# Two more gates in a pair, a denser plan for the second mixer, and three pieces of work moved ahead of their waits

## The chip, the cores and the metric

The kernel runs on one core of a Trainium2 chip. The metric is the device time of one execution in microseconds; the figure for a kernel is the median of its runs. The kernel before takes 2862.22 us (three runs, 2858.88 to 2863.82).

## What is computed

One layer of a hybrid decoder, for a prompt of 512 tokens and eight sequences that each add one token. The 520 token columns go through the dense products together. Two token mixers work on the same normalised input, and sigmoid gates merge them; a feed-forward block with a short convolution follows. Cut to what the change touches:

```
mq, mk, mv, mo, mi, mf, fq, fk, fv, ff, ga, gb = split(h @ w_in + b_in)
y_m = mlstm_output(mlstm_fn(q_m, k_m, v_m, ig, lf_m), mo)        # first mixer
q_f, k_f = rmsnorm(fq), rmsnorm(fk); v_f = fv; lf_f = log_sigmoid(ff)
y_f = fox_fn(q_f, k_f, v_f, lf_f)                                # second mixer (FoX), 8 heads of 128
merged = sigmoid(ga) * (y_m @ w_proj_a) + sigmoid(gb) * (y_f @ w_proj_b)
x = x + g1 * (merged @ w_out)
h2 = modulate(rmsnorm(x, norm2_w), sh2, sc2)
a, g = split(h2 @ w_ffn_in)                                      # 2048 -> 2 x 5632
x = x + g2 * ((gelu(conv3(a)) * g) @ w_ffn_out)
```

In the second mixer a prompt token attends to the prompt tokens before it, with a bias from summed log forget values. A sample token attends to 256 past rows, which lie in two pages of 128 rows of a cache (`cache_k`, `cache_v`) that a page table points into, and to itself. `gb` has 2048 channels: 16 tiles of 128 channels, called gates here.

## The kernel before, in words

**Dense products.** Every fp32 operand is split into a high and a low part, and a product is three matmuls (high by high, high by low, low by high). The 520 columns are two halves of 260. For one tile of 128 output channels, `dense` (L196) goes over 16 tiles of 128 input channels: 16 x 3 x 2 = 96 matmuls of 128x260. ScalarE casts a block of 1024 weight columns to its high part `wh` and VectorE subtracts to get the low part `wl` (L167, L168), from a block `raw` that SyncE's queue loads.

**Pairs.** Most products are done by `run_pairs` (L326): two output tiles and two column halves are treated as a 2x2 block product and computed with seven products of 24 matmuls instead of eight. VectorE pays for it with sums of weight blocks (`raw<-raw,raw`) and of results (`tg`, `tt`, `at`). A unit is seven steps, and `late` maps a step to extra work that is issued there. The results of a product of a unit stand in PSUM banks `x`, `y` and `z`; a later product of the unit may write a bank again only when VectorE or ScalarE has read it.

**The second mixer beside the gates.** `NB2` of the 16 gates are computed in pairs, the rest by `dense` in the loop at L1762. `dense` calls `step()` after each of the 16 input tiles, and a step takes the next entry of the list `bg`, which is a plan of the second mixer: entry s holds the functions that are issued after s steps. A step is six matmuls. The plan is written by `put(s, f)` (L1701 to L1732); a scheduler may let an instruction stand later than its step where what it needs comes later. For each of the eight heads, spaced `HP` steps apart from b = 1 + HP*head, the plan issues:

- `f_load` (L1432): five loads `fi` on SyncE's queue; `f_norm` (L1437): two VectorE products `fi<-fi,qwc,fi` and `fi<-fi,nkw,fi`, and a store of the keys by GpSimd (`out_kT`);
- `f_split`: high and low parts, the low parts `fql`, `fkl` on GpSimd; `f_forget` (`nFb`), `f_values` (`vtp`, then `fvl` on VectorE);
- `f_scores` (L1563): four score blocks `fS` on TensorE, softmax on VectorE and ScalarE (`fs`, `sm`); `f_turn` (L1584): transposes `fPT` of the softmax; `f_attend` (`fy`).

For the eight sample tokens the plan issues, sixteen times, `s_load` (L1620): one broadcast load `qb` of the query row from the DRAM scratch `dqf`, on SyncE's queue, and two indirect loads `kp` of a page of keys by GpSimd (`gather`, L868); and `s_scores` (L1630): for each page a product `kp<-kp,qb` and a sum `sc<-kp`, in program order on VectorE. `s_rows` (L1613) writes `dqf` from a transpose `qSt`. After the last score come a softmax (`sS`), its transpose `sPT` (L1659), a `memset` of `pp` on GpSimd, and 32 indirect loads `vp` of pages of values (`s_gather`); each page feeds two matmuls `sO` (`s_attend`, L1682) and then `sOT` and sums into `yS`. `y_split` and `y_sample` make the mixer's result `yf` ready for the product with `w_proj_b` (`pb`).

**The start of the feed-forward block.** `W2` is the last unit of the product with `w_out`. `features(e, z)` (L2098) makes eight input tiles of one column half: for each tile VectorE scales `xa` by the row factor `rr`, the sample columns get a sum (by VectorE for the first tile, by GpSimd for the others), ScalarE writes the high part `bf`, VectorE the low part. Its dictionary `between` names other work that is issued after tile j. `half_norm(z)` makes `rr` of a column half from four sums `ms` on TensorE, through ScalarE and VectorE. `beside` takes the input tiles in turn for several products: `fa` and `fg` are the two halves of FFN unit 0, `fb` is the first of unit 1. Pairs of FFN tiles follow (L2512); `sum_parts(n)` makes eight split tiles from sums of input tiles (eight ScalarE casts `bf<-xa`, eight VectorE differences), and `whole_copy`, `whole_conv`, `whole_gate` finish a tile that was computed without pairing.

**Order on an engine.** Each engine, and SyncE's and GpSimd's queues, runs its instructions in the order in which they stand; an instruction that waits holds all behind it on its engine.

Of the kernel before, what the change touches and what calls it, by code (L numbers as in the profile page):

```python
# [63 lines left out]
def tile_hybrid_step(ctx: ExitStack, tc: tile.TileContext, I, O):  # L64
# [1547 lines left out]

    def s_rows(e):  # L1613
        ps = mm_ps("qSt")
        T.transpose(ps[:32, :P], qS[:, e].rearrange("p b h -> p (b h)"), ident)
        qrow = pt("qrow")
        V.tensor_copy(qrow[:32, :P], ps[:32, :P])
        nc.sync.dma_start(dqf[e].rearrange("b (h d) -> (b h) d", h=4), qrow[:32, :P])

    def s_load(i):  # L1620

        e, b = divmod(i, NS)
        qb = pt("qb")
        nc.sync.dma_start(qb[:, :512], dqf[e, b].partition_broadcast(P))
        kps = [pt("kp") for _ in range(NPG)]
        W.k[i] = qb, kps
        for g, kp in enumerate(kps):
            gather(kp[:, :512], I["cache_k"], idx_h[e][:, b * NPG + g:b * NPG + g + 1])
# [991 lines left out]
```

## Time and profile before

| | before |
|---|---|
| median of three runs | 2862.22 us |
| the profiled execution | 2862.7 us |
| its span, first to last instruction | 2861.0 us |
| TensorE busy | 2825.4 us, 99% |
| VectorE busy | 2154.0 us, 75% |
| ScalarE busy | 1360.5 us, 48% |
| GpSimd busy | 413.3 us, 14% |
| granted TensorE clock, mean | 0.997 |

Times in the text are microseconds from the start of the span. The stages that the change touches: pairs up to 1004.2; the dense gates with the second mixer to about 1215; the products with `w_proj_b` and `w_out` to 1476; the start of the feed-forward block to 1552; then its pairs. In rows of the trace PE is TensorE (PEld its weight loads), DVE VectorE, ACT ScalarE, POOL GpSimd, SP SyncE. A row of a timeline has start, length, engine, line, operation, output and inputs, size and count, and in brackets the idle time just ahead of it and what ended that. Matmul rows overlap: a 128x260 matmul lasts 0.28 us, but the next begins 0.12 us later.

### The profile page before, as it was taken

How to read it: one execution, taken by the hardware profiler on the slowest of the kernel's cores; microseconds unless marked ns; L12 is line 12 of the kernel's file. 1: busy time of each engine (PE TensorE's matmuls, PEld its weight loads, DVE VectorE, ACT ScalarE, POOL GpSimd, SP SyncE). 2: the span in 40 equal slices, each digit the busy share in tenths (PEclk: the TensorE clock that was granted, in tenths of full speed). 3: DMA queues.
4: the chain of work that ended last, by engine and by line, in shares of the span. 5: the costliest groups of instructions: out<-in, count | busy, mean ns of one | idle time of the engine just before them, and what ended most of it. 6: DMA issues, size and time to landing. Idle time of an engine off the chain costs nothing.

```text
span 2861.0 us, 57607 instructions
## 1 busy us (share of the span) xinstructions
PE 2825.4 (99%) x23318; PEld 2711.8 (95%) x23318; DVE 2154.0 (75%) x3318; ACT 1360.5 (48%) x2131; POOL 413.3 (14%) x687
## 2 busy tenths in 40 slices
PE   8999999999999999999999999999999999999999
PEld 6888998999999989799999999999999999999999
DVE  5986764676777759468888887878787888788787
ACT  4335543455455544444555444444444445544543
POOL 0001110211100145402111010101010101100100
PEclk9999999999999999999999999999999999999999
DMA  9946657945555578576772344444343346745753
GB/s 339 308 143 201 232 178 261 302 166 188 195 182 175 182 246 270 183 235 208 216 249 93 127 143 129 156 130 159 129 146 117 127 141 188 208 155 169 189 160 104
DMA packets 226755, 531.44 MB, mean 186 GB/s; under 512 B 30304, under 2 KB 83024, under 8 KB 226488
## 3 DMA queue, kind: packets, MB, share of 16 engines
q1 hardware_dynamic: 187296, 426.89, 46.2%
q0 software_dynamic: 38752, 100.64, 11.5%
q8 instruction: 183, 3.00, 0.4%
q14 instruction: 84, 0.69, 0.1%
q10 hardware_dynamic: 440, 0.23, 0.0%
HBM read 451.28 MB, written 72.92 MB: 183 GB/s over the span
## 4 chain that ended last, share of the span: by engine, by line
PE 85%; DVE 5%; issue 5%; DMA 2%; ACT 2%; POOL 1%; SPq 0%; POOLq 0%; DVEq 0%; ACTq 0%
PE x L60 33%; PE y L60 17%; PE z L60 8%; PE gate L213 4%; PE pre L60 3%; PE fo L60 3%; PE pa L213 3%; PE mo L213 2%; PE adp L60 2%; PE mv L213 2%; PE adp L409 1%; DVE wl L60 1%; PE mq L213 1%; PE mk L213 1%; ACT wh L60 1%
## 5 line engine op out<-in xcount | busy, mean ns | idle before, releaser
L60 DVE TENSOR_TENSOR wl<-raw,wh 128x1024 fp32r<-128x1024 f32 (+1 forms) x666 | 802.1, 1205 | 353.3 <-ACT wh L60 348.6
L60 ACT CAST wh<-raw 128x1024 fp32r<-128x1024 f32 (+1 forms) x666 | 689.5, 1036 | 754.7 <-DVE raw L60 386.3
L60 PE MATMUL x<-bf,wh 128*128 128x260 f32 x2624 | 475.2, 282 | 2.1 <-DVE tg L60 2.1
L60 DVE TENSOR_TENSOR raw<-raw,raw 128x1024 f32<-128x1024 f32 x339 | 413.7, 1220 | 5.8
L60 PEld LDWEIGHTS x<-bf,wh 128*128 128x128 f32 x2624 | 403.3, 188 | 2.2 <-ACT wh L60 2.2
L60 PE MATMUL x<-bf,wl 128*128 128x260 f32 x1312 | 370.0, 282 | 0.0
L60 PEld LDWEIGHTS x<-bf,wl 128*128 128x128 f32 x1312 | 246.8, 188 | 0.0
L60 PE MATMUL y<-bf,wh 128*128 128x260 f32 x1312 | 238.2, 282 | 0.0
L60 PEld LDWEIGHTS y<-bf,wh 128*128 128x128 f32 x1312 | 201.6, 188 | 0.0
L168 DVE TENSOR_TENSOR wl<-raw,wh 128x1024 fp32r<-128x1024 f32 x92 | 113.1, 1229 | 107.8 <-ACT wh L167 105.0
L60 PE MATMUL x<-ff,wh 128*128 128x260 f32 x1024 | 186.1, 283 | 0.0
L60 PE MATMUL x<-hf,wh 128*128 128x260 f32 x1008 | 185.4, 284 | 0.0
L60 PE MATMUL y<-bf,wl 128*128 128x260 f32 x656 | 184.7, 282 | 0.0
L167 ACT CAST wh<-raw 128x1024 fp32r<-128x1024 f32 x92 | 96.4, 1048 | 162.0 <-DMA raw<-in_w_in 43.4
L60 PEld LDWEIGHTS x<-hf,wh 128*128 128x128 f32 x1008 | 155.0, 188 | 13.4 <-issue 7.5
L60 PEld LDWEIGHTS x<-ff,wh 128*128 128x128 f32 x1024 | 157.6, 188 | 0.0
L60 PE MATMUL x<-ff,wl 128*128 128x260 f32 x512 | 144.6, 282 | 0.0
L60 PE MATMUL x<-hf,wl 128*128 128x260 f32 x504 | 142.2, 282 | 0.0
L60 PE MATMUL fo<-fe,wh 128*128 128x260 f32 x768 | 125.6, 284 | 1.1 <-DVE fo L60 0.9
L60 PEld LDWEIGHTS y<-bf,wl 128*128 128x128 f32 x656 | 123.5, 188 | 0.0
L60 PE MATMUL z<-bf,wh 128*128 128x260 f32 x656 | 120.9, 284 | 0.0
L60 PEld LDWEIGHTS fo<-fe,wh 128*128 128x128 f32 x768 | 105.6, 188 | 2.5 <-DVE fo L60 2.1
(642 smaller groups left out, 7076.9 us busy)
## 6 DMA issues: line engine op xcount, KB each, us to landing
raw<-in_w_fi SPq DMA_DIRECT2D x176, 512.0 KB
raw<-in_w_in SPq DMA_DIRECT2D x155, 512.0 KB
ar<-in_w_ada SPq DMA_DIRECT2D x192, 256.0 KB
raw<-in_w_ada SPq DMA_DIRECT2D x96, 512.0 KB
raw<-in_w_fo SPq DMA_DIRECT2D x64, 512.0 KB
raw<-in_w_out SPq DMA_DIRECT2D x32, 512.0 KB
raw<-in_w_fo SPq DMA_DIRECT2D x32, 384.0 KB
dff<-cc POOLq DMA_DIRECT2D x44, 260.0 KB
```

Of the source, the lines that this page charges most:

```text
L60: return lambda *a, **k: self.tc.keep_in_program_order(getattr(self.eng, op)(*a, **k))
L167: S.copy(wh[:, :n], raw[:, :n])
L168: V.tensor_tensor(wl[:, :n], raw[:, :n], wh[:, :n].bitcast(F32), op=ALU.subtract)
L213: T.matmul(acc[:, z, :HN], a[:, o], b[:, z * HN:(z + 1) * HN], start=(k == 0 and i == 0), stop=(k == K - 1 and i == 2))
L409: ins = T.matmul(ps[32 * g:32 * g + 32, :], cs[:, k, :], w, start=first, stop=last, tile_position=(0, 32 * g))
```

## The change

1. `NB2` goes from 4 to 6: two more gates are computed in a pair, and the dense loop has 10 gates (160 steps) instead of 12 (192 steps).
2. The plan of the second mixer is written for 160 steps: a head every 18 steps instead of 22, a score load every 5.5 steps instead of 7, the softmax of the sample at 104 instead of 127, the attends at 113 + 4n instead of 137 + 5n.
3. `s_rows` for both halves and `s_load` for the first two score loads move out of the plan into the last pair unit (steps t0 + 10 and t0 + 12), so that GpSimd's first four page loads stand ahead of its store of head 0's keys.
4. At the start of the feed-forward block, `features(0, 1)` gets another order of the work between its tiles (the last unit of `w_out` and the weights of unit 1 earlier), VectorE instead of GpSimd makes the sample sum of tiles 1 and 2, and the first product of unit 1 (`fb`, second column half) is interleaved with `fa` and `fg` instead of standing behind them; `half_norm(0)` now stands behind six input tiles of three products, where it stood behind four of two.
5. In the first FFN pairs, `sum_parts(7)` goes from step 1 to step -1 and `sum_parts(4)` from step 4 to step 1.

The diff, cut to its core:

```diff
-    NB2 = 4
+    NB2 = 6
...
-                  t0 + 9: lambda: (hX.pop(5), f_load(heads[0])), t0 + 13: on(f_norm, heads[0])}
+                  t0 + 9: lambda: (hX.pop(5), f_load(heads[0])), t0 + 10: lambda: (s_rows(0), s_rows(1)),
+                  t0 + 12: lambda: (s_load(0), s_load(1)), t0 + 13: on(f_norm, heads[0])}
...
-    HP = 22
+    HP = 18
...
-        put(6 + 7 * i, s_load, i)
-        put(18 + 7 * i, s_scores, i)
+        if i > 1:
+            put(6 + 11 * i // 2, s_load, i)
+        put(17 + 11 * i // 2, s_scores, i)
...
-        t = 137 + 5 * n
+        t = 113 + 4 * n
...
-                    (V if i == 0 else G).tensor_tensor(u[:, SEQ:N], u[:, SEQ:N], ada[:, b0 + i, 1:9], op=ALU.add)
+                    (V if i < 3 else G).tensor_tensor(u[:, SEQ:N], u[:, SEQ:N], ada[:, b0 + i, 1:9], op=ALU.add)
...
-    features(0, 1, {0: lambda: W2.end(0), 2: lambda: W2.end(1), 3: lambda: half_squares(0),
-                    4: lambda: cast(1, 0, 0), 6: lambda: low(ws)})
+    features(0, 1, {0: lambda: (W2.end(0), cast(1, 0, 0)), 1: lambda: W2.end(1), 2: lambda: low(ws),
+                    4: lambda: half_squares(0)})
     load2(0, 0, 1)
     some = [(0, 0, ws[0]), (0, 1, ws[1])]
-    beside(some, 0, 1, range(4))
+    beside(some, 0, 1, range(3))
+    acc.append([[None, mm_ps("fb")[:, :HN]], [None, None]])
+    beside([(1, 0, ws[2])], 0, 1, range(3))
+    beside(some + [(1, 0, ws[2])], 0, 1, range(3, 6))
     half_norm(0)
-    acc.append([[mm_ps("fb")[:, :HN] for z in range(2)] for o in range(2)])
-    beside(some, 0, 1, range(4, 8))
+    acc[1][0][0] = mm_ps("fb")[:, :HN]
+    acc[1][1] = [mm_ps("fb")[:, :HN] for z in range(2)]
+    beside(some + [(1, 0, ws[2])], 0, 1, range(6, 8))
     fetch_xa(range(8, KC - 2))
-    eight(1, 0, 0, (1,), ws[2])
     features(0, 0)
     beside(some, 0, 0)
     eight(1, 0, 0, (0,), ws[2])
...
-    run_pairs(units, {-2: lambda: eight(2, 1, 1, (0, 1), w), -1: lambda: whole_copy(2),
-                         1: lambda: sum_parts(7), 2: lambda: whole_conv(2), 3: lambda: whole_gate(2),
-                         4: lambda: sum_parts(4),
+    run_pairs(units, {-2: lambda: eight(2, 1, 1, (0, 1), w), -1: lambda: (whole_copy(2), sum_parts(7)),
+                         1: lambda: sum_parts(4), 2: lambda: whole_conv(2), 3: lambda: whole_gate(2),
```

Three places show what moves. First, VectorE at the start of the second mixer, before (`kp<-kp,qb` and `sc<-kp` are score load 0, `fi_12187` is head 1's query, `fs` and `sm` head 0's softmax):

```order
L225 TENSOR_TENSOR fvl_12176<-vtp_12170,fvh_12175 128x384
L168 TENSOR_TENSOR wl_12421<-raw_12418,wh_12420 128x1024
L60 TENSOR_TENSOR kp_12205<-kp_12205,qb_12203 128x512
L60 TENSOR_REDUCE sc<-kp_12205 128x4
L60 TENSOR_TENSOR kp_12206<-kp_12206,qb_12203 128x512
L1439 SCALAR_TENSOR_TENSOR fi_12187<-fi_12187,qwc,fi_12189 128x520
L1575 ISA fs_12236,sm_12237<-fS_12233,nfb_12148 128x128
L1575 ISA sm_12237 128x1
```

and now (`fi_12404` and `fi_12405` are head 1's query and key):

```order
L60 TENSOR_TENSOR kp_12272<-kp_12272,qb_12270 128x512
L60 TENSOR_REDUCE sc<-kp_12272 128x4
L60 TENSOR_TENSOR kp_12273<-kp_12273,qb_12270 128x512
L60 TENSOR_REDUCE sc<-kp_12273 128x4
L168 TENSOR_TENSOR wl_12692<-raw_12689,wh_12691 128x1024
L1464 SCALAR_TENSOR_TENSOR fi_12404<-fi_12404,qwc,fi_12406 128x520
L1464 SCALAR_TENSOR_TENSOR fi_12405<-fi_12405,nkw,fi_12407 128x520
L225 TENSOR_TENSOR fvl_12426<-vtp_12420,fvh_12425 128x384
L1601 ISA fs_12470,sm_12471<-fS_12467,nfb_12388 128x128
```

The score products still stand ahead of head 0's softmax, but their pages are asked for in the last pair unit; both of head 1's products now stand ahead of the softmax as well.

Second, TensorE late in the second mixer, before: the rows that end with pages 24 to 27 of the 32 (`vp`, counted from 0 in GpSimd's order).

```order
L213 MATMUL gate_14391<-hh_1193,wh_14394 128x260 x2
L213 MATMUL gate_14391<-hl_1194,wh_14394 128x260 x2
L213 MATMUL gate_14391<-hh_1193,wl_14395 128x260 x2
L1194 MATMUL fS_14515<-fkh_14339,fqh_14335 128x512
L1194 MATMUL fS_14515<-fkl_14340,fqh_14335 128x512
L1194 MATMUL fS_14515<-fkh_14339,fql_14336 128x512
L1572 LDWEIGHTS identb
L1572 MATMUL fS_14515<-mask_f,identb 128x128
L1682 MATMUL sO_14527<-vp_14365,pp_12109 32x512
L1682 MATMUL sO_14527<-vp_14386,pp_12109 32x512
L1682 MATMUL sO_14527<-vp_14411,pp_12109 32x512
L1682 MATMUL sO_14527<-vp_14422,pp_12109 32x512
```

and now, pages 20 to 22:

```order
L213 MATMUL gate_14312<-hh_882,wl_14316 128x260 x2
L1689 MATMUL sO_14360<-vp_14296,pp_12359 32x512
L1689 MATMUL sO_14360<-vp_14307,pp_12359 32x512
L213 MATMUL gate_14312<-hh_1173,wh_14315 128x260 x2
L213 MATMUL gate_14312<-hl_1174,wh_14315 128x260 x2
L213 MATMUL gate_14312<-hh_1173,wl_14316 128x260 x2
L213 MATMUL gate_14312<-hh_1193,wh_14315 128x260 x2
L213 MATMUL gate_14312<-hl_1194,wh_14315 128x260
L1689 MATMUL sO_14360<-vp_14333,pp_12359 32x512
```

Where four pages stood together behind some steps of other work, single pages now stand a step and a half apart. Counted over the whole order, 219 gate matmuls stand between the transpose `sPT` and the last `sO` before, and 110 now.

Third, VectorE in `features(0, 1)`, before (`bf_18047`, `bf_18052`, `bf_18057` are the low parts of tiles 0, 1 and 2; `wl_18076` is unit 1's weight, which stood after tile 4's low part):

```order
L60 SCALAR_TENSOR_TENSOR bf_18047<-xa_17817,ada,bf_18047 128x260
L60 TENSOR_TENSOR xa_17821<-xa_17821,rr_16009 128x260
L60 TENSOR_TENSOR tt_17810<-z_17777,tt_17810 128x260
L60 SCALAR_TENSOR_TENSOR x_17771<-tt_17810,ada,x_17771 128x260
L60 TENSOR_TENSOR xa_17823<-xa_17823,rr_16009 128x260
L60 SCALAR_TENSOR_TENSOR bf_18052<-xa_17819,ada,bf_18052 128x260
L60 TENSOR_TENSOR xa_17825<-xa_17825,rr_16009 128x260
L60 SCALAR_TENSOR_TENSOR bf_18057<-xa_17821,ada,bf_18057 128x260
```

and now (`bf_18049`, `bf_18057`, `bf_18066` are tiles 0, 1 and 2, `wl_18053` unit 1's weight):

```order
L60 SCALAR_TENSOR_TENSOR bf_18049<-xa_17819,ada,bf_18049 128x260
L60 TENSOR_TENSOR tt_17812<-z_17779,tt_17812 128x260
L60 SCALAR_TENSOR_TENSOR x_17773<-tt_17812,ada,x_17773 128x260
L60 TENSOR_TENSOR xa_17823<-xa_17823,rr_16011 128x260
L60 TENSOR_TENSOR xa_17823<-xa_17823,ada 128x8
L60 TENSOR_TENSOR wl_18053<-raw_17968,wh_18052 128x1024
L60 TENSOR_TENSOR xa_17825<-xa_17825,rr_16011 128x260
L60 SCALAR_TENSOR_TENSOR bf_18057<-xa_17821,ada,bf_18057 128x260
L60 TENSOR_TENSOR xa_17827<-xa_17827,rr_16011 128x260
L60 SCALAR_TENSOR_TENSOR bf_18066<-xa_17823,ada,bf_18066 128x260
```

The weight's low part moves ahead of tile 1's, and a sample sum stands behind the scaling of tile 2 (and of tile 1).

More of the change, by code (lines that the diff above doesn't have):

```diff
@@ L1426, in rows_make, with s_rows, s_load @@
                                 x[:, o:o + 32].rearrange("p (h b) -> p h b", h=4), w, None, op0=ALU.mult)
+    dqf = dram([2, NS, 4 * P], "dqf")
+    def s_rows(e):
+        ps = mm_ps("qSt")
+        T.transpose(ps[:32, :P], qS[:, e].rearrange("p b h -> p (b h)"), ident)
+        qrow = pt("qrow")
+        V.tensor_copy(qrow[:32, :P], ps[:32, :P])
+        nc.sync.dma_start(dqf[e].rearrange("b (h d) -> (b h) d", h=4), qrow[:32, :P])
+    def s_load(i):
+        e, b = divmod(i, NS)
+        qb = pt("qb")
+        nc.sync.dma_start(qb[:, :512], dqf[e, b].partition_broadcast(P))
+        kps = [pt("kp") for _ in range(NPG)]
+        W.k[i] = qb, kps
+        for g, kp in enumerate(kps):
+            gather(kp[:, :512], I["cache_k"], idx_h[e][:, b * NPG + g:b * NPG + g + 1])
+    class Pages:
+        pass
+    W = Pages()
+    W.v, W.k = {}, {}
     root = {}
@@ L1606, in f_attend @@
         H.vt = H.last = H.y = None
-    dqf = dram([2, NS, 4 * P], "dqf")
     sc = mconst([P, NPG, NS, FH], "sc", tag="m1")
@@ L1611, in tile_hybrid_step @@
     yS = mconst([P, NS, FH], "yS")
[L1613 to L1628, printed above, removed]
     def s_scores(i):
@@ L1666, in s_weights @@
         W.pz = pz
-    W = Head()
     def s_gather(i):
@@ L1697, in s_heads @@
                             ps[:, h4 * P:(h4 + 1) * P].rearrange("p (b i) -> p b i", b=4)[:, :, hh], op=ALU.add)
-    W.v, W.k = {}, {}
     plan = {}
@@ L1716, in tile_hybrid_step @@
         if hh:
-            put(b - 18, f_load, H)
+            put(b - 16, f_load, H)
             put(b, f_norm, H)
@@ L1727, in tile_hybrid_step @@
             put(b + 26 + j, f_attend, H, j)
-        put(max(148 + 4 * hh, b + 31), y_split, hh)
-    for e in range(2):
-        put(0, s_rows, e)
+        put(max(124 + 4 * hh, b + 31), y_split, hh)
     for i in range(16):
-        put(6 + 7 * i, s_load, i)
-        put(18 + 7 * i, s_scores, i)
-    put(126, s_bias)
-    put(127, s_softmax)
-    put(131, s_weights)
+        if i > 1:
+            put(6 + 11 * i // 2, s_load, i)
+        put(17 + 11 * i // 2, s_scores, i)
+    put(103, s_bias)
+    put(104, s_softmax)
+    put(108, s_weights)
     for i in range(8):
-        put(126 + i, s_gather, i)
+        put(103 + i, s_gather, i)
     for n in range(8):
-        t = 137 + 5 * n
+        t = 113 + 4 * n
         put(t, s_attend, n)
@@ L1744, in tile_hybrid_step @@
         if n % 2:
-            put(t + 7, s_heads, n // 2)
+            put(t + 6, s_heads, n // 2)
     for hh in range(FH):
-        put(183 if hh < FH - 1 else 188, y_sample, hh)
+        put(152 if hh < FH - 1 else 159, y_sample, hh)
     def run(fs):
```

## The prediction

> **What bounds the kernel now.** I read the page first, then the waits of TensorE, then windows and timelines at the places that the diff touches.
>
> ```profile
> span 2861.0 us, 57607 instructions
> ...
> PE 2825.4 (99%) x23318; PEld 2711.8 (95%) x23318; DVE 2154.0 (75%) x3318; ACT 1360.5 (48%) x2131; POOL 413.3 (14%) x687
> ```
>
> TensorE is busy 99% of the span, so a change gains in two ways only: fewer matmuls, or less of the 35.6 us in which TensorE waits. The waits of TensorE, in total, times and longest, say where those are:
>
> ```profile
> PE fPT L1590 <- DVE fs L1579: 5.2, 4, 3.2
> ...
> PE x L60 <- DVE tg L60: 2.1, 1, 2.1
> ...
> PE fa L60 <- DVE bf L60: 1.4, 3, 0.6
> ...
> PE fa L60 <- ACT bf L60: 1.1, 1, 1.1
> ...
> PE sO L1682 <- DMA vp<-in_cache_v,idx: 0.4, 1, 0.4
> ...
> PE sPT L1659 <- DVE pp L1654: 0.3, 1, 0.3
> ```
>
> The first four rows are what the three moves aim at, 9.8 us together. In the mixer nothing else waits worth naming: `sO`, which waits for pages, has 0.4 us. For the price of a matmul and the load of the mixer, windows with busy time and count per engine (PE, PEld, DVE, ACT, POOL), clock, DMA share and GB/s:
>
> ```profile
> 700.00:750.00 50.00, 50.00 (x415) 47.07 (x414) 34.19 (x35) 24.53 (x40) 7.01 (x13) 1.00 0.53 175
> ...
> 1050.00:1100.00 50.00, 49.61 (x399) 48.00 (x398) 40.85 (x96) 23.74 (x51) 25.92 (x25) 1.00 0.81 266
> 1100.00:1150.00 50.00, 49.72 (x399) 47.83 (x397) 43.18 (x91) 23.20 (x50) 25.38 (x24) 1.00 0.70 238
> ```
>
> Among the pairs 415 matmuls fill 50 us: 0.1205 us each. In the mixer VectorE is busy 84.0 of 100 us. It is not the bound, but it is near.
>
> **Gates, -2.9 us.** Two gates cost 2 x 96 = 192 matmuls dense and 7 x 24 = 168 in a pair: 24 fewer, 24 x 0.1205 = 2.9 us. The pair's extra sums of weights and results fall on VectorE, 34.19 of 50 us busy among the pairs; that hides them, and without that cover they would cost what they last, 1.2 us a block. Certain to a few tenths.
>
> **Start of the mixer, -4.0 us.** Head 0's softmax stands on VectorE behind score load 0, and that waits for pages:
>
> ```profile
> 1012.59 1.05 POOL L868 DMA_INDIRECT kp<-in_cache_k,idx  x1 [0.15 <-issue]
> ...
> 1018.27 0.69 DVE L60 TENSOR_TENSOR kp<-kp,qb 128x512 f32<-128x512 f32 x1 [3.39 <-DMA kp<-in_cache_k,idx]
> ...
> 1021.75 0.69 DVE L60 TENSOR_TENSOR kp<-kp,qb 128x512 f32<-128x512 f32 x1 [2.06 <-DMA kp<-in_cache_k,idx]
> ...
> 1023.03 0.28 DVE L1575 CUSTOM_DVE_ANT_0 fs<-fS,nfb 128x128 f32<-128x128 f32 x1
> ```
>
> VectorE is idle 3.39 + 2.06 = 5.45 us for two pages, and TensorE then waits at `fPT`. Asked for in the last pair unit, the pages are there. Late next is head 1's first product, `fi<-fi,qwc,fi`: it and its sister now stand ahead of the softmax, and its five loads stand on SyncE's queue. It ran at 1022.36 before with no wait of its own; I allow 1.2 us of the 5.2 to remain. Ends: 0 (the wait only changes its name) and -5.2. On the queues that the moved work passes, GpSimd and SyncE, four page loads and two `qb` loads now stand among the pair's stores, where GpSimd is busy 7.01 of 50 us. The two transposes `qSt` now stand in the pair unit and may wait for VectorE; the trace has no such wait, the nearest row is that of `sPT`: **+0.3**, ends 0 and 1.
>
> **The pages of values, +4.8 us.** This is the term that I find only by counting. The rows by line for GpSimd from the `memset` to the last page (busy, mean | idle ahead):
>
> ```profile
> L868 POOL DMA_INDIRECT vp<-in_cache_v,idx x25 | 27.0, 1078 | 7.3 <-issue 5.8 <-DVE yS L1661 0.3 <-PE fy L1194 0.3
> L225 POOL TENSOR_TENSOR fql<-fi,fqh 128x512 fp32r<-128x512 f32 x2 | 2.6, 1308 | 4.1 <-PE gate L213 2.4 <-issue 1.7
> L225 POOL TENSOR_TENSOR fkl<-fi,fkh 128x512 fp32r<-128x512 f32 x2 | 2.5, 1270 | 0.0
> L1767 POOL DMA_DIRECT2D dsg<-sgm x2 | 1.2, 590 | 3.6 <-ACT sgm L1766 3.6
> L1440 POOL DMA_DIRECT2D out_kT<-fi x1 | 0.6, 588 | 0.0
> L1663 POOL MEMSET pp<- 128x512 f32 x1 | 0.5, 542 | 0.0
> ```
>
> A page takes (27.0 + 7.3)/25 = 1.37 us of GpSimd's time. In both orders 24 pages stand behind the `memset`, with the same other work: 24 x 1.37 + 2.6 + 2.5 + 1.2 + 0.6 + 0.5 = 40.3 us, so the last begins 38.9 us after the `memset`. And a page is there late after its row begins:
>
> ```profile
> 1146.88 0.31 PE L1659 MATMUL sPT<-ident,pp 64*128 64x64 f32 x2 [0.28 <-DVE pp L1654]
> ...
> 1153.91 1.05 PE L1682 MATMUL sO<-vp,pp 128*32 128x512 f32 x2 [0.36 <-DMA vp<-in_cache_v,idx]
> ...
> 1201.59 1.06 PE L1682 MATMUL sO<-vp,pp 128*32 128x512 f32 x8
> ```
>
> ```profile
> 1147.94 1.85 POOL L868 DMA_INDIRECT vp<-in_cache_v,idx  x1 [0.30 <-DVE yS L1661]
> ```
>
> ```profile
> 1191.08 0.95 POOL L868 DMA_INDIRECT vp<-in_cache_v,idx  x1 [0.30 <-issue]
> ```
>
> ```profile
> 1196.36 0.14 PEld L1682 LDWEIGHTS sO<-vp,pp 128*32 128x32 f32 x2 [0.51 <-DMA vp<-in_cache_v,idx]
> ```
>
> Page 7 took 1153.91 - 1147.94 = 6.0 us to its reader, page 27 1196.36 - 1191.08 = 5.3. With 5.6, and 0.6 from `sPT` to the `memset`, the last page arrives no sooner than 0.6 + 38.9 + 5.6 = 45.1 us after `sPT`. Before, TensorE took 1201.59 - 1146.88 = 54.7 us for that stretch, which hid it. Now 109 gate matmuls fewer stand in it: 54.7 - 109 x 0.1205 = 41.6 us. TensorE waits 3.5 us more, and with some idle of GpSimd's own (it had 7.7 us at `fql` and `dsg`, which I cut to 1.3 because TensorE is now the one that waits) 4.8. Ends: 0, and 3.5 + 7.7 = 11.2.
>
> [...]
>
> **VectorE in the mixer, +1.5 us.** A head's period was 22 steps x 0.72 = 15.9 us of gates and about 5.9 of its own matmuls, and is now 13.0 + 5.9 = 18.9. VectorE's share, at 84% of 21.8, was 18.3 us; its head work is the same, the scores 18/5.5 against 22/7, so 18.3 again, 97% of 18.9. It also idles for the heads' loads:
>
> ```profile
> L1439 DVE SCALAR_TENSOR_TENSOR fi<-fi,qwc,fi 128x520 f32<-128x520 f32 x7 | 5.3, 757 | 9.5 <-DMA fi<-drr 9.1 <-issue 0.4
> ```
>
> That is 1.4 us a head: 19.7 against 18.9, so VectorE falls behind by 0.8 us a head over five heads, 4 us. The new order lets the softmax transposes of heads 3 to 5 stand up to twelve steps after their place in the plan, 8.7 us, which covers it; what is not covered I put at 1.5. Ends 0 and 9. The last step of the plan is 159 of 160 where it was 188 of 192; the first `pb` product needs head 7 only at its end, and that hides it; uncovered it would cost 1 to 2 us.
>
> **Feed-forward features, +2.8 us.**
>
> ```profile
> 1475.81 0.43 DVE L60 TENSOR_TENSOR xa<-xa,rr 128x260 f32<-128x260 f32 x1
> ...
> 1479.03 0.48 DVE L60 SCALAR_TENSOR_TENSOR bf<-xa,ada,bf 128x260 fp32r<-128x260 f32 x1
> ...
> 1482.45 1.23 DVE L60 TENSOR_TENSOR wl<-raw,wh 128x1024 fp32r<-128x1024 f32 x1 [0.45 <-ACT wh L60]
> ```
>
> ```profile
> 1484.93 0.46 ACT L60 ACTIVATE rr<-ms,eps 128x260 f32<-128x260 f32 x1
> ...
> 1487.73 1.94 ACT L60 ACTIVATE bf<-xa,ada 128x260 fp32r<-128x260 f32 x4 [1.89 <-DVE xa L60]
> ```
>
> Tile 1's low part, at 1479.03, now stands behind the 1.2 us `wl` and two short sums, 1.5 us later. TensorE works in order and cannot reach unit 1's products meanwhile; they close the later waits instead (0.6 and what `ms` left), so about +0.8 of this stays. The rest is `half_norm(0)`. From ScalarE's first `rr` to the first `bf` of the next half are 1487.73 + 0.5 - 1484.93 = 3.3 us, and 0.3 ahead of that. Before, 48 matmuls stood between `ms` and that half; now 18 do, 18 x 0.1205 = 2.2 us. TensorE waits 3.6 - 2.2 = 1.4 us, and 0.6 more for the first low part. Ends -1.2 (the interleaving fills half of the 2.5 us of `fa` waits, as it may be meant) and +3.5.
>
> **sum_parts, -2.1 us.**
>
> ```profile
> 1552.65 1.23 DVE L60 TENSOR_TENSOR wl<-raw,wh 128x1024 fp32r<-128x1024 f32 x1 [3.25 <-ACT wh L60]
> ...
> 1567.59 2.79 DVE L60 TENSOR_TENSOR bf<-xa,bf 128x260 fp32r<-128x260 f32 x8
> 1570.31 0.41 DVE L60 TENSOR_TENSOR tg<-x,tt 128x260 f32<-128x260 f32 x1
> ```
>
> `tg`, for which TensorE waits 2.1 us, stands behind eight differences of 2.79 us. They move up; the earliest eight go where VectorE idled 3.25 us ahead of 1552.65. `tg` comes 2.7 us sooner and nothing else was near. Ends -1 and -2.1.
>
> **The sum.** -2.9 - 4.0 + 0.3 + 4.8 + 1.5 + 2.8 - 2.1 = +0.4. The profiled execution took 2862.7 us (span 2861.0 and 1.7 around it), 0.5 above the median of the runs; the sum is a difference, so I set it on the median: 2862.22 + 0.4 = **2862.6**. About 0.2%, 5.7 us, is what a measurement of this kernel can tell from no change: faster is below 2856.5, slower above 2867.9.
>
> **Rivals.** *VectorE becomes the bound in heads 1 to 5 (slower).* For it: 97% and the idle for loads; against it: the late order. It decides once VectorE and its waits take more than 18.9 + 8.7/5 = 20.6 us a head. With 2 us more of waits for the head loads, which SyncE's queue holds behind weight loads, the deficit is 5 x (21.7 - 18.9) = 14 us less 5 covered, +9 where I have +1.5: 2870.1.
>
> *The pages do not bind and the features gain (faster).* For it: the `sO` row shows 0.4 us; against it: the count above. With 0 for the pages and -1.2 for the features: 2862.6 - 4.8 - 4.0 = 2853.8.
>
> *The start does not do what it says:* head 1's loads take the place of the pages and the 4.0 us stay. For it: the order shows both products ahead of the softmax; against it: no wait at 1022.36. 2866.6.
>
> **Chances.** The forecast 0.47, VectorE 0.24, the faster rival 0.19, the start 0.10. Faster 0.20 (that rival and 0.01 of the forecast's spread), slower 0.27 (VectorE, and 0.03 of the start's upper part), same 0.53. The range goes from 2855 to 2871: it leaves out about half of the faster rival and the upper ends of the pages and of VectorE.
>
> **What would show it.** Right: no `fPT` wait over 1 us near head 0; `sO` waits for `vp` of 3 to 8 us in all; a wait of 2 us at the second `fa` tile and one of 1.4 at the first `fa` of the next half; no wait for `tg`. Wrong: `sO` without waits, `fPT` or `fS` waits at heads 1 to 5 above 3 us in all, or `features` with less idle than the 2.5 us that it has.

## The result: 1.0% slower, and the profile after

The changed kernel takes 2890.65 us (median of four runs, 2889.57 to 2893.43), the kernel before beside it 2863.02 (four runs): a ratio of 1.0100, 95% interval 1.0088 to 1.0113. The forecast was 2862.6, and the slower end of its range 2871. The profiled execution took 2889.6 us. The page, for the rows that the prediction began with:

```profile
span 2887.9 us, 57587 instructions
...
PE 2836.4 (98%) x23294; PEld 2715.7 (94%) x23294; DVE 2161.3 (75%) x3330; ACT 1363.1 (47%) x2137; POOL 409.0 (14%) x687
```

The 24 matmuls are gone (23318 to 23294), and still TensorE is busy 11 us longer: its clock is part of the answer. TensorE's waits:

```profile
PE fy L1194 <- DVE fpl L225: 8.2, 4, 4.1
...
PE fS L1194 <- ACT last L1583: 5.7, 1, 5.7
PE sO L1689 <- DMA vp<-in_cache_v,idx: 4.4, 1, 4.4
...
PE fa L60 <- DVE bf L60: 2.8, 3, 2.3
PE fS L1194 <- POOL fkl L225: 2.4, 1, 2.4
PE fa L60 <- ACT bf L60: 2.4, 2, 1.3
...
PE x L60 <- ACT tg L60: 0.7, 1, 0.7
```

`fPT` (5.2 us before) and `tg` (2.1) are gone as forecast, and 4.4 us at `vp` and 2.3 at the second feature tile are there as forecast. Not forecast are `fy`, and `fS` twice: 16.3 us. (`fpl` is the low part of the turned softmax; `last` is ScalarE's copy of a head's last block of values.) By stages, from the first starts in the timelines:

| from, to | before | after | difference | by count of matmuls |
|---|---|---|---|---|
| start, first `nFb` | 1008.3 | 1028.1 | +19.8 | +168 x 0.1205 = +20.2 |
| first `nFb`, first `pb` (the mixer) | 211.4 | 214.8 | +3.4 | -192 x 0.1205 = -23.1 |
| first `pb`, first `fa` | 257.3 | 256.8 | -0.5 | 0 |
| first `fa`, last `fg` (features) | 74.3 | 79.7 | +5.4 | 0 |
| last `fg`, end | 1309.7 | 1308.5 | -1.2 | 0 |

So the mixer lost 26.5 us against the count. Three things in it can be read off. TensorE's idle time went from 6.4 to 20.8 us (+14.4). The clock is the second. Windows of 4 us in the first head, with busy time and count per engine, clock, DMA share and GB/s:

```profile
1040.00:1044.00 4.00, 2.79 (x18) 2.42 (x17) 0.53 (x1) 0.00 (x0) 0.00 (x0) 0.88 0.82 246
1044.00:1048.00 4.00, 0.00 (x0) 0.00 (x0) 1.35 (x3) 0.00 (x0) 0.07 (x1) 0.98 0.75 258
1048.00:1052.00 4.00, 3.55 (x13) 2.94 (x14) 2.68 (x17) 1.36 (x5) 0.52 (x1) 0.50 0.18 69
1052.00:1056.00 4.00, 4.00 (x26) 4.00 (x25) 2.77 (x6) 2.94 (x6) 0.56 (x1) 0.67 0.09 13
1056.00:1060.00 4.00, 4.00 (x36) 3.96 (x35) 2.48 (x5) 2.07 (x4) 2.27 (x3) 1.00 0.87 259
```

After the wait TensorE runs 13 and 26 matmuls in 4 us where 36 are usual: the granted clock is 0.50 from 1047.82 to 1054.65. The trace's clock records have stretches of 3.41 or 6.83 us at exactly 0.50. In the mixer there are 17.1 us of them, behind four of the waits, where before it was one of 6.83 us behind the wait for `fPT`; half of the busy part of these is 8.0 us against 2.9 (+5.1). The third is the pages' products. TensorE's `sO` rows:

```profile
1196.81 1.91 PE L1689 MATMUL sO<-vp,pp 128*32 128x512 f32 x10
...
1199.14 1.05 PE L1689 MATMUL sO<-vp,pp 128*32 128x512 f32 x2
...
1200.38 1.05 PE L1689 MATMUL sO<-vp,pp 128*32 128x512 f32 x2
```

One page (x2) lasts as long as four had lasted together in the prediction's row at 1201.59 (x8, 1.06 us). From each start to the next start, the 64 records take 13.8 us before and 18.8 after without the waits; about 1.2 of the 5.0 is the half clock, counted above: +3.8. Together 23.3 of the 26.5; some 3 us are spread over the other forms. The 13.8 us before hold waits too, which TensorE's rows hide: four of its eight groups of four pages take 1.0 us, and the other four 2.1 to 3.0, in each of which a weight load waits for a page:

```profile
PEld sO L1682 <- DMA vp<-in_cache_v,idx: 2.5, 4, 1.3
```

**Why VectorE was late.** It is busy less than before, 76 of the 100 us from 1050 to 1150 where it was 84. What ended its longer idle times:

```profile
1043.47 0.76 DVE L1464 SCALAR_TENSOR_TENSOR fi<-fi,qwc,fi 128x520 f32<-128x520 f32 x1 [8.06 <-DMA fi<-drr]
1046.87 0.76 DVE L1464 SCALAR_TENSOR_TENSOR fi<-fi,nkw,fi 128x520 f32<-128x520 f32 x1 [2.65 <-DMA fi<-drr]
...
1112.31 0.69 DVE L60 TENSOR_TENSOR kp<-kp,qb 128x512 f32<-128x512 f32 x1 [4.45 <-DMA kp<-in_cache_k,idx]
```

It waits for loads, not for its own work. Head 1's loads stood here on SyncE's queue:

```profile
1026.43 1.28 SPq L161 DMA_DIRECT2D raw<-in_w_in  x2
1036.90 0.33 SPq L1441 DMA_DIRECT2D qb<-dqf  x1
1037.28 0.42 SPq L1460 DMA_DIRECT2D fi<-dqk  x1
1037.79 0.41 SPq L1460 DMA_DIRECT2D fi<-drr  x1
```

The row at 1036.90 is the query row of score load 3. It takes a buffer of the last pair, and waits for a store to give it back. From the waits of SyncE's queue:

```profile
SPq L1441 <- DMA dsg<-tt: 9.0, 1, 9.0
```

Head 1's five loads `fi` stand behind it. Head 0's softmax stands on VectorE behind head 1's two products.

The page of keys at 1112.31 is a matter of order alone. GpSimd asks for the pages of loads 8, 9 and 10 in this order (`kp_13109` is load 8, `kp_13263` load 10):

```
L868 DMA kp_13109<-in_cache_k,idx_2456 128x512
L868 DMA kp_13110<-in_cache_k,idx_2456 128x512
L868 DMA kp_13152<-in_cache_k,idx_2456 128x512
L868 DMA kp_13153<-in_cache_k,idx_2456 128x512
L868 DMA kp_13263<-in_cache_k,idx_2456 128x512
L868 DMA kp_13264<-in_cache_k,idx_2456 128x512
```

and VectorE reads them in this one:

```
L60 TENSOR_TENSOR kp_13263<-kp_13263,qb_13261 128x512
L60 TENSOR_TENSOR kp_13264<-kp_13264,qb_13261 128x512
L60 TENSOR_TENSOR kp_13109<-kp_13109,qb_13107 128x512
L60 TENSOR_TENSOR kp_13110<-kp_13110,qb_13107 128x512
L60 TENSOR_TENSOR kp_13152<-kp_13152,qb_13150 128x512
L60 TENSOR_TENSOR kp_13153<-kp_13153,qb_13150 128x512
```

The load asked for last is read first, 8.4 us after its issue, with two older loads waiting behind it. In the dense plan four loads of keys are read so (3, 7, 10 and 13), and one group of pages of values: pages 12 to 15 are read ahead of 8 to 11, and the 4.4 us at `vp` are that group's. Before, no read ran ahead of its place where it cost a wait.

**The features.** TensorE at the first two tiles:

```profile
1499.74 0.39 PE L60 MATMUL fa<-bf,wh 128*128 128x260 f32 x1 [1.13 <-ACT bf L60]
...
1503.81 0.59 PE L60 MATMUL fa<-bf,wh 128*128 128x260 f32 x1 [2.29 <-DVE bf L60]
...
1505.06 0.64 PE L60 MATMUL fa<-bf,wh 128*128 128x260 f32 x2
```

The waits of `fa` and `fg` are 6.6 us where they were 3.5, and from 1501.79 on 6.83 us run at half speed (0.64 us for two matmuls that otherwise take 0.40): 2.4 us more. The two make the 5.4 us.

### The profile page after: what moved, and what is told of

It is laid out like the page before. It is cut to its first block, busy times and chain, and to the rows that moved or that the text cites. A ratio compares the mean times of both kernels' runs of the same rounds, so it can differ in the third digit from the quotient of the medians.

```text
span 2887.9 us, 57587 instructions
## 1 busy us (share of the span) xinstructions
PE 2836.4 (98%) x23294; PEld 2715.7 (94%) x23294; DVE 2161.3 (75%) x3330; ACT 1363.1 (47%) x2137; POOL 409.0 (14%) x687
## 4 chain that ended last, share of the span: by engine, by line
PE 88%; DVE 5%; DMA 3%; ACT 2%; issue 2%; POOL 0%; SPq 0%; DVEq 0%; ACTq 0%; POOLq 0%
PE x L60 34%; PE y L60 17%; PE z L60 8%; PE fo L60 3%; PE pa L213 3%; PE pre L60 3%; PE pb L213 3%; PE gate L213 3%; PE mo L213 2%; PE adp L60 2%; PE mv L213 2%; PE adp L409 1%; DVE wl L60 1%; PE mq L213 1%; DMA ar<-in_w_ada 1%
## 5 line engine op out<-in xcount | busy, mean ns | idle before, releaser
L60 DVE TENSOR_TENSOR wl<-raw,wh 128x1024 fp32r<-128x1024 f32 (+1 forms) x673 | 810.5, 1205 | 356.0 <-ACT wh L60 351.8
L60 PE MATMUL x<-hf,wh 128*128 128x260 f32 x1056 | 194.2, 284 | 0.0
L60 PEld LDWEIGHTS x<-hf,wh 128*128 128x128 f32 x1056 | 162.3, 188 | 13.4 <-issue 7.5
L60 PE MATMUL x<-hf,wl 128*128 128x260 f32 x528 | 148.9, 282 | 0.0
```

The source lines that it names most:

```text
L60: return lambda *a, **k: self.tc.keep_in_program_order(getattr(self.eng, op)(*a, **k))
```

## The experiments

Each kernel ran beside the kernel before, in five rounds, each of four sets on a chip of its own. Medians of the kernel before were 2863.5, 2861.1, 2862.8 and 2860.6 us in these sets, so sets are compared by their ratios; 0.1% is 2.9 us.

### Which part costs what

**e1**, the start undone:

```diff
-  t0 + 10: lambda: (s_rows(0), s_rows(1)), t0 + 12: lambda: (s_load(0), s_load(1)),
+  for e in range(2): put(0, s_rows, e)
-        if i > 1:
-            put(6 + 11 * i // 2, s_load, i)
+        put(6 + 11 * i // 2, s_load, i)
```

> The changed kernel with only the early start undone: s_rows and score loads 0 and 1 are back in the plan (steps 0, 6 and 11). Theory A (the early start delays head 1 by a chain of buffers, and that is one loss among several): the three waits of 2.4, 5.7 and 1.2 us in the first two heads and their half-speed clock (about 4 us) go, the old wait at head 0's transposes (about 5 us and 2.6 of slow clock) comes back; 2885, some 6 us under the changed kernel, and the waits for fpl in heads 2 to 4 stay. Rival B (the late head 0 pushes every later head, so that the start is the whole loss): 2866 to 2870, and the fpl waits go too. Rival C (the start gained what was forecast, the dense plan alone makes the waits): 2894 to 2897.

2882.36 us, 1.0058 (1.0045 to 1.0071): 8 us less by the medians and 12 by the ratios. That is theory A in its sign and nearly in its time, and the start is a loss inside the dense plan. Not all of theory A came: the waits of 2.4 and 5.7 us went, but the old wait at `fPT` did not come back (0.5 us), and the waits at `fpl` grew from 8.2 to 12.3 us. The two profiled executions differ by 6.2 us, of which 3.5 lie in the mixer and 2.0 behind the features, so that the trace places only a part of the 8 to 12 us.

**e2**, item 4 of the change taken back (the order of `features(0, 1)`, `beside` and `half_norm(0)`).

```diff
-    features(0, 1, {0: lambda: (W2.end(0), cast(1, 0, 0)), 1: lambda: W2.end(1), 2: lambda: low(ws),
+    features(0, 1, {0: lambda: W2.end(0), 2: lambda: W2.end(1), 3: lambda: half_squares(0),
...
```

> The changed kernel with only the order at the start of the feed-forward block undone. Theory A (the new order costs its two waits of 2.3 and 1.3 us and a stretch at half clock behind them): 5 us under the changed kernel, 2885. Rival (the stretch there takes longer only because of what the mixer left in the queues): within 1.5 us of the changed kernel.

2886.55 us, 1.0080 (1.0067 to 1.0093): 4 to 6 us less, as expected. The stage takes 75.0 us (79.7 in the changed kernel, 74.3 in the kernel before).

**e3**, items 1 and 2 alone, on the kernel before.

```diff
-    NB2 = 4
+    NB2 = 6
...
-    HP = 22
+    HP = 18
...
```

> The kernel before with the two more gates in a pair and the dense plan alone; start, features and sum_parts as before. Theory A (the dense plan by itself leaves VectorE's operands too little lead, so that it waits for head loads and pages, and single pages cost TensorE more than four together): 18 us over the kernel before, 2881, with fpl or fS waits over 5 us in heads 1 to 5, a wait for vp of 3 us or more, and stretches at half clock. Rival B (the start is the whole loss): 2860 to 2863, without fpl waits.

2882.87 us, 1.0069 (1.0056 to 1.0082): 19.4 us more than the kernel before. Its waits:

```profile
PE fy L1194 <- DVE fpl L225: 12.7, 7, 5.8
...
PE sO L1689 <- issue: 4.4, 1, 4.4
```

Theory A. VectorE's idle times ahead of these are 6.0, 7.7 and 3.0 us at pages of keys, each a load that is read out of its order.

**e4**, item 3 alone, on the kernel before.

```diff
+  t0 + 10: lambda: (s_rows(0), s_rows(1)), t0 + 12: lambda: (s_load(0), s_load(1)),
...
-        put(6 + 7 * i, s_load, i)
+        if i > 1:
+            put(6 + 7 * i, s_load, i)
```

> The kernel before with the early start alone: four gates in pairs, the old plan, but s_rows and score loads 0 and 1 in the last pair unit. Theory A (the chain of buffers: qrow's store, a page load, the stores of the last pair, a qb load, head 1's loads): VectorE waits over 5 us for head 1's loads and TensorE over 4 us in heads 0 and 1; 2866 to 2870. Rival C (the early start gains by itself, and only the dense plan spoils it): 2858 to 2860, no wait over 1.5 us in heads 0 and 1.

2864.98 us, 0.9999 (0.9990 to 1.0007): no change. Neither theory: the waits in head 0 are 1.9 us at `fkl` and 2.1 at `fPT`, 4.0 where they were 4.8, with as much half-speed time (6.83 us). A wait went and another took its place. Why the same move costs 8 to 12 us in the dense plan, where head 1 stands four steps earlier, is not settled.

### Why the dense plan waits

**e5**, the scores of the sixteen loads pinned behind each other, so that VectorE reads in the order of the loads:

```diff
-        v = Ordered(tc, nc.vector)
+        v = After(tc, nc.vector, W)
...
+            if getattr(self.w, "last", None):
+                self.tc.add_manual_dep(ins.ins, self.w.last, mybir.DependencyInfo(
+                    mybir.DependencyClass.NoSync, mybir.DependencyReason.DATA), reason="after")
+            self.w.last = ins.ins.name
```

> The changed kernel, with the score products and sums of the sixteen score loads pinned behind each other, so that VectorE reads the loads in the order in which GpSimd asks for their pages (in the changed kernel load 10 is read ahead of loads 8 and 9, load 13 ahead of 11 and 12, and loads 3 ahead of 1 and 2). Theory O (the inverted order is what makes VectorE wait for pages of keys, 4.45 and 1.05 us, and TensorE then for fpl, 4.07 and 0.77, with a half-speed stretch of about 2 us behind): all four go, 2883 to 2885. Rival Q (the loads are late as such because their buffers come free late, so that VectorE waits as long for another page): kp waits of 4 us and more stay, 2889 to 2891.

2882.25 us, 1.0076 (1.0063 to 1.0088): 7 to 8 us less. No wait for a page of keys is left, which is theory O. But 1.0 to 4.4 us at `fpl` stay in heads 3 to 5, now behind loads of heads, and the pins also brought four pages of values together again, so that a part of the gain is `sO`'s (13.3 us without waits, for 18.8). Windows of heads 1 to 3, here:

```profile
1060.00:1120.00 60.00, 58.27 (x453) 55.01 (x452) 56.36 (x122) 26.59 (x61) 27.35 (x28) 1.00 0.78 251
```

and in the changed kernel:

```profile
1060.00:1120.00 60.00, 52.54 (x400) 50.10 (x400) 43.37 (x93) 23.66 (x52) 25.59 (x26) 0.97 0.78 244
```

With its operands in order VectorE is busy 56.4 of 60 us in this stretch, 94%, where it had been 72%. There the prediction's 97% was a limit close behind the one that bound; from 1120 to 1160 VectorE is busy 77%.

**e6**, the 32 pages of values pinned in their order on GpSimd's queue, and each group's products issued last page first, so that they stand together:

```diff
-        for b4 in range(4):
+        for b4 in (3, 2, 1, 0):
...
+            if b4 < 3:
+                tc.keep_in_program_order(ins)
...
-        gather(W.v[i][:, :512], ...)
+        tc.keep_in_program_order(gather(W.v[i][:, :512], ...))
```

> The changed kernel, with the 32 loads of pages of values pinned in their order on GpSimd's queue, and with the four sO products of a group issued last page first, so that they stand together. Theory G (a page alone costs TensorE 0.98 us, four together 1.0, and the one wait of 4.4 us for vp is another inverted order): the sO products fall from 18.3 to about 10 to 13 us, the wait and its half-speed stretch of 1.3 us go, 2879 to 2882. Rival P (the prediction's: GpSimd's 24 loads bind, so that TensorE, with less work of its own in between, waits for the last page of each group): vp waits of 5 us and more in all, 2886 to 2891.

2898.39 us, 1.0129 (1.0114 to 1.0144): 8 us slower, outside both ranges. Of theory G the products came true (11.6 us for 18.8), of rival P the waits:

```profile
PE sO L1689 <- DMA vp<-in_cache_v,idx: 8.5, 3, 3.5
```

44 us of the mixer run at half speed, for 17. Apart the pages cost TensorE 0.98 us each, together they make it wait.

**e7**, items 1 and 2 with the mends of e5 and e6, and item 5; on e3's kernel:

```diff
+        v = After(tc, nc.vector, W)
...
+        for b4 in (3, 2, 1, 0):
...
+        tc.keep_in_program_order(gather(W.v[i][:, :512], ...))
```

> The two more gates in a pair, the dense plan and the sum_parts move, with scores in order and pages grouped as in the two runs above; start and features as in the kernel before. Theories O and G together: from 2882.9 (gates alone) less 1.4 for sum_parts, about 14 for the waits behind inverted key pages with their slow clock, and 5 to 9 for the pages of values: 2855 to 2862, fpl waits under 2 us in all. Rival V (VectorE, at 97% of a head's period, is the bound once it does not wait for pages): fpl or fPT waits of 6 us and more stay, 2867 to 2874.

2879.95 us, 1.0066 (1.0054 to 1.0078): 1 to 3 us less than the gates alone, outside both ranges. 9.0 us at `vp` and 10.2 at `fpl` stand in place of the waits removed, 24 us at half speed. The `fpl` waits over 6 us are rival V's sign; the 9.0 us at `vp` are in neither account.

**e9**, head 1's loads ahead on SyncE's queue:

```diff
-  t0 + 12: lambda: (s_load(0), s_load(1)),
+  t0 + 12: lambda: (s_load(0), s_load(1), f_load(heads[1])),
```

> The changed kernel, with head 1's five loads asked for in the last pair unit as well, so that on SyncE's queue they stand ahead of the query rows of score loads 2 and 3 (in the changed kernel they stand behind load 3's row, which waits 9.0 us for a store of the last pair to give its buffer back). Theory A (that place in the queue is what makes VectorE wait 8.1 and 2.7 us for head 1's loads, and TensorE 5.7 us at fS): those waits go, with a half-speed stretch of about 3 us; 2881 to 2884. Rival (head 1 is late for want of its own buffers or of DMA bandwidth): fS waits over 4 us stay, 2889 to 2892.

2890.63 us, 1.0103 (1.0088 to 1.0117): nothing gained. The place in the queue was real, the cure was not:

```profile
PE fS L1194 <- POOL fkl L225: 6.1, 1, 6.1
...
PE fS L1194 <- DVE sbias L1564: 2.2, 1, 2.2
```

5.7 us at `last` became 6.1 at `fkl` and 2.2 at `sbias` (VectorE's copy of the bias for the sample scores). GpSimd's rows show where the 6.1 us come from:

```profile
1035.85 1.22 POOL L868 DMA_INDIRECT kp<-in_cache_k,idx  x1 [6.50 <-DVE sc L60]
...
1039.61 1.27 POOL L225 TENSOR_TENSOR fql<-fi,fqh 128x512 fp32r<-128x512 f32 x1
...
1042.36 1.35 POOL L225 TENSOR_TENSOR fkl<-fi,fkh 128x512 fp32r<-128x512 f32 x1
```

A load of a page of keys waits 6.5 us for a buffer that a score sum on VectorE gives back, and head 0's low parts stand behind it on GpSimd. The changed kernel has the same order in a milder form:

```profile
1025.36 0.94 POOL L868 DMA_INDIRECT kp<-in_cache_k,idx  x1 [8.94 <-DMA dqf<-qrow]
...
1030.51 1.20 POOL L868 DMA_INDIRECT kp<-in_cache_k,idx  x1 [1.46 <-DMA qb<-dqf]
...
1036.27 1.27 POOL L225 TENSOR_TENSOR fkl<-fi,fkh 128x512 fp32r<-128x512 f32 x1
```

The early start's fourth page load waits 8.9 us for the store of the query rows, the pair's stores and the next page loads stand behind it, and `fkl` begins 8.2 us after the first `nFb`. In the kernel before both low parts stood ahead of the pages, and `fkl` began 2.9 us after `nFb`. From 1030 to 1040 the DMA engines are busy 1.02 of the time (0.99 in the changed kernel); whether the loads also hold each other back is not shown.

**e12**, e5 with the products of a group together, and the heads' loads on ScalarE's queue:

```diff
-            nc.sync.dma_start(t[:, :N], src)
+            nc.scalar.dma_start(t[:, :N], src)
```

> The changed kernel with scores in load order, the four sO products of a group issued last page first, and all heads' loads issued by ScalarE's queue instead of SyncE's. Theory L (in the dense plan heads' loads stand in SyncE's queue behind query rows and weight blocks that wait for VectorE, while VectorE waits for them): the waits of VectorE for fi fall from 18 us in the run with scores in order to under 5, TensorE's fS and fpl waits from 15 to under 4; 2866 to 2872. Rival V (VectorE's own work, 97% of a head's period, is the bound): the fpl waits stay over 6 us in all, with VectorE busy over 90% in heads 1 to 5; 2878 to 2884.

2877.87 us, 1.0056 (1.0043 to 1.0069): 13 us less than the changed kernel, 4 to 6 less than e5, and short of theory L's range, at the edge of rival V's. TensorE's long waits are gone, short ones stay:

```profile
PE fy L1211 <- DVE fpl L242: 5.9, 6, 1.7
...
PE sO L1706 <- DMA vp<-in_cache_v,idx: 2.8, 2, 2.4
```

None of them lasts over 2.4 us, and yet 20 us of the mixer run at half speed. Theory L's own sign did not come: VectorE still waits 18.4 us for loads `fi` (19.3 in e5), in ten waits of at most 4.7 us where there were five of up to 8.0. So SyncE's queue alone is not what makes the heads' loads late.

**f3**, e12 with the start and the features of before.

```diff
+  for e in range(2): put(0, s_rows, e)
...
+    features(0, 1, {0: lambda: W2.end(0), 2: lambda: W2.end(1), 3: lambda: half_squares(0),
...
```

> Six gates in pairs and the dense plan, with the start and the features as before, sum_parts moved, scores in load order, the pages' products four together and the heads' loads on ScalarE's queue: the run with loads on ScalarE less the features' 4 us and the start. If VectorE's 95% of a head's period bounds the dense plan (theory V): fpl waits of 5 us and more stay, with half-speed stretches, 2869 to 2875. If only the queues' orders were wrong (theory O with L): waits under 3 us in the mixer, 2858 to 2863.

2872.65 us, 1.0042 (1.0028 to 1.0056), in theory V's range. The profiled execution is the slowest of the five, 2879.3 us, with 27 us of the mixer at half speed:

```profile
PE sO L1706 <- DMA vp<-in_cache_v,idx: 8.0, 3, 4.0
...
PE fS L1211 <- ACT last L1600: 6.2, 1, 6.2
PE fy L1211 <- DVE fpl L242: 6.0, 5, 2.5
```

The best order that was tried for the two gates still costs 12 us. That VectorE's work is what is left is not shown: it is busy 93% of the time from 1060 to 1100 here, and 75% from 1100 to 1160, and its longest wait is one of 13.7 us for a query row, ahead of head 0's softmax and of the 6.2 us at `last`:

```profile
1043.36 0.69 DVE L71 TENSOR_TENSOR kp<-kp,qb 128x512 f32<-128x512 f32 x1 [13.71 <-DMA qb<-dqf]
```

### Features, sums and the clock

**e8**, the low part of unit 1's weight back behind tile 4.

```diff
-                    2: lambda: low(ws), 4: lambda: half_squares(0)})
+                    4: lambda: (low(ws), half_squares(0))})
```

> The changed kernel with one move in the feed-forward features undone: the low part of unit 1's weight is made after tile 4 again instead of after tile 2, all else of the new order kept. Theory (the prediction's: tile 1's low part stands behind the 1.2 us of wl, and that is the 2.3 us wait, which also halves the clock for some 6 us): wait under 1 us, no half-speed stretch there, 2886 to 2888; the 1.3 us wait behind half_norm stays. Rival (the wait only goes to the first fb product, which needs that weight): 2890 to 2892.

2890.00 us, 1.0103 (1.0089 to 1.0116): no gain. The wait fell from 2.3 to 1.2 us, so its cause was as forecast, but the 6.83 us at half speed stayed, behind 1.1, 0.4 and 1.2 us of idle time. The time lies in the rival's range, but the wait at `fb` that the rival names is not in the profile.

**e10**, the early start with head 1's loads ahead, and the `sum_parts` move, on the kernel before; **e11**, the `sum_parts` move alone. e10 has both parts of this, e11 the second:

```diff
+  t0 + 10: lambda: (s_rows(0), s_rows(1)), t0 + 12: lambda: (s_load(0), s_load(1), f_load(heads[1])),
...
-  -1: lambda: whole_copy(2), 1: lambda: sum_parts(7),
+  -1: lambda: (whole_copy(2), sum_parts(7)), 1: lambda: sum_parts(4),
```

> The kernel before (four gates in pairs, old plan, old features) with the early start, head 1's loads in the last pair unit as above, and the sum_parts move. Theory A: no wait over 1.5 us at fPT or fS in heads 0 and 1, so no half-speed stretch there (3 us before), no tg wait; 5 to 8 us under the kernel before, 2854 to 2857. Rival (a start that saves its wait loses as much to another one, as in the start alone, which came out even): 2860 to 2862.

> The kernel before with the sum_parts move alone. The prediction's term: tg's wait of 2.1 us goes and 0.7 of another wait stands behind it, with no half-speed stretch in either: 1.4 to 2.1 us under the kernel before, 2859 to 2860; by the verdict's measure no change.

e10: 2861.90 us, 1.0001 (0.9992 to 1.0010); 6.4 us at `fkl` and 1.2 at `sbias` stand for the 4.8 at `fPT`, and the rival holds. e11: 2859.48 us, 0.9991 (0.9983 to 1.0000), `tg`'s wait gone and 0.7 us behind it, as forecast.

**f1** and **f2** put matmuls of the identity, which nothing reads, into unused columns of a PSUM bank, ahead of waits: in f1 18 in the first head and 6 behind the first feature tile of the changed kernel, in f2 14 ahead of `fPT` of head 0 in e11's kernel. Theory K, in both, is that the half-speed stretch behind such a wait goes when TensorE's idle time ahead of it is filled.

```diff
+    def fill(n):
+        for _ in range(n):
+            tc.keep_in_program_order(nc.tensor.matmul(spare[0][:, 0, 384:512], ident, ident, start=False, ...))
...
+    put(20, fill, 14)
```

> The changed kernel with matmuls of the identity that nothing reads, put ahead of three of its waits: 6 and 12 in the first head (ahead of the waits of 2.4 and 5.7 us at fS), 6 behind the first feature tile (ahead of the 2.3 us wait). Each wait is ended by another engine at the same time as without them. [...] Rival (the half speed does not cost, or comes from something else): stretches and time stay, 2890 to 2894.

> The kernel before with the sum_parts move and 14 such matmuls ahead of its one wait in the mixer (1.3 and 3.2 us at fPT of head 0), which a half-speed stretch of 6.8 us follows. Theory K: the stretch goes, 2.9 us less than sum_parts alone, 2855 to 2858, faster than both kernels. Rival: 2859 to 2862.

f1: 2889.77 us, 1.0099 (1.0084 to 1.0115), next to the rival's range. The stretches at 1037 and 1502 are gone, and the features stage is 2.1 us shorter (77.6 for 79.7). But behind the wait at `vp` a stretch of 6.83 us now stands for one of 3.41: the mixer has 17.1 us at half speed as before, and pays for 18 matmuls more. One stretch more or less in one execution proves little, though: e2 and e8 leave the plan of the mixer as the changed kernel has it, and have 20.5 us. f2: 2854.84 us, 0.9983 (0.9974 to 0.9992), theory K. Windows at head 0, in e11:

```profile
1020.00:1030.00 10.00, 5.11 (x37) 4.40 (x36) 9.47 (x29) 4.15 (x10) 4.22 (x5) 0.90 0.94 349
1030.00:1040.00 10.00, 10.00 (x63) 9.83 (x62) 3.49 (x6) 4.92 (x10) 3.87 (x4) 0.76 0.71 204
```

and in f2:

```profile
1020.00:1030.00 10.00, 8.70 (x75) 8.46 (x73) 8.03 (x27) 4.15 (x10) 4.29 (x5) 1.00 1.01 373
1030.00:1040.00 10.00, 8.86 (x70) 8.69 (x71) 5.05 (x10) 4.83 (x10) 4.65 (x5) 1.00 0.88 260
```

The clock stays at 1.00, the waits at `fPT` are 2.4 us where they were 5.3, and the mixer takes 205.8 us where it took 210.6 in e11. f2 is the fastest kernel here, faster than both that were given, by 0.17% than the kernel before (0.08 to 0.26). Between it and e11 alone the intervals overlap, so that the profile, and not the times, is the evidence for the fill.

## Why the prediction was wrong, step by step

- **Gates, -2.9:** right; 24 matmuls fewer at the same price (414 in 50 us among the pairs).
- **Start, -4.0:** wrong. The step that failed is "I allow 1.2 us of the 5.2 to remain": alone the move gained nothing (e4), in the dense plan it costs 8 to 12 us (e1). The prediction saw that head 1's products and loads come next and put no price on where those loads stand: 9.0 us behind a row that waits for a buffer. Nor did moving them help (e9). For the moved page loads on GpSimd's queue it allowed +0.3; that they would stand ahead of head 0's low parts, and wait there, was not in it: `fkl` costs TensorE 2.4 us in the changed kernel, 1.9 in e4, 6.1 in e9 and 6.4 in e10.
- **Pages of values, +4.8:** the wait is 4.4 us, but that is luck: it is one group read out of order, not the count of GpSimd's time. Waits like those that the count stands for came where the products stand in groups (2.8 us in e12, 8.0 in f3, 8.5 in e6, 9.0 in e7, within the ends of 0 and 11.2); that GpSimd's count sets them is not shown. The order listing of the second place showed pages apart, and the 0.98 us that each then costs TensorE was not counted: +3.8. Nor does the row of 0.4 us mean that the kernel before hardly waited for pages: its weight loads did, 2.5 us in four waits.
- **VectorE, +1.5:** this is the other step that failed. It compared busy sums (18.3 against 18.9 us a head) and took the idle time at loads as a constant 1.4 us a head. In the new order that idle time grew instead: at `fi` from 9.5 to 20.4 us over seven heads. The row of the changed kernel for the query product and that for the key product:

```profile
L1464 DVE SCALAR_TENSOR_TENSOR fi<-fi,qwc,fi 128x520 f32<-128x520 f32 x7 | 5.3, 758 | 15.8 <-DMA fi<-drr 15.8
L1464 DVE SCALAR_TENSOR_TENSOR fi<-fi,nkw,fi 128x520 f32<-128x520 f32 x7 | 5.3, 753 | 4.6 <-DMA fi<-drr 4.6
```

The rival "VectorE becomes the bound" had the place and the sign, at 2870 (it subtracts 5 us for the late order, where the term itself had 8.7); its cause came second, behind loads out of order, which are 7 to 8 us (e5). With items 1 and 2 alone, the pages of values and the clock among them, the loss is 19.4 us. Why VectorE still waits some 18 us for heads' loads, on either queue (e5, e12), stays open.
- **Features, +2.8:** both waits came in their size (2.3 for 2.0, 1.3 for 1.4), and e8 shows the cause of the first. The term of 5.4 has 2.4 us of half speed that was not priced.
- **sum_parts, -2.1:** right in kind; 1.4 by the waits, since 0.7 us of another wait stood behind it (e11's interval is 0 to 4.9 us).
- **The clock** has no term at all (the prediction's "a change gains in two ways only" leaves it out), though the kernel before has its 6.83 us at half speed behind the wait that the prediction quoted, and the mean of 0.93 stood in the window from 1000 to 1050. It makes +5.1 in the mixer and +2.4 in the features.

## What to carry to other kernels

Where a plan is made denser, match each queue's order of issue with its readers' order, and ask of every load what it stands behind and which buffer it waits for: loads read out of order cost 7 to 8 us here (e5), with VectorE at 72%, and a page load that waited 8.9 us on GpSimd's queue held back head 0's low parts behind it (`fkl` 8.2 us after `nFb`, where it had been 2.9). A busy share says what an engine could do, not when its operands come. And price a wait together with the clock behind it: with waits of 1.1, 0.4 and 2.3 us within 5.2 us at the first feature tiles came 6.83 us at half speed, and 14 matmuls that nothing reads were worth their time ahead of one wait (f2: the mixer 205.8 us for 210.6), though 24 in other places were not (f1: 2889.77 us for 2890.65).
